# Gate and up of two pairs of 256 features in each FFN, as seven products of blocks in place of eight

## The chip, the core and the metric

The kernel runs on one core of a Trainium2 chip. The metric is the device time of one execution, in microseconds; it stands as the median of three runs. The engines are PE (TensorE: matmuls; PEld is its weight load), DVE (VectorE), ACT (ScalarE), POOL (GpSimd) and SP (SyncE, which issues most loads). Each engine works through its own instructions in the order of the program.

## What is computed

256 rows of 1024 features, in f32, go through an SSM layer, an attention layer and twice through FFN, hybrid mixer, FFN. The change is in the four FFNs, which are:

```python
D_FF = 2816
def swiglu(x, w_gate, w_up, w_down):
    return (jax.nn.silu(x @ w_gate) * (x @ w_up)) @ w_down
...
x = x + 0.5 * swiglu(rmsnorm(x, ffn1_norm[l]), ffn1_w_gate[l], ffn1_w_up[l], ffn1_w_down[l])
```

## The kernel before

**Products in three parts.** A weight is loaded as f32 ("raw"), and split into a high part (`whi`, an ACT cast to f32r) and a low part (`wlo = raw - whi`, a DVE subtraction). `mm3` (L195) forms one product as three matmuls, high x high, high x low, low x high.

**Weight units.** All weights of the layers after the SSM are cut into units of 1 MB (2048 elements in each of 128 partitions), in the order in which they are used. `converting` (L101) is a generator over them: a unit is split in four quarters, with a cast of 512 for each quarter and a low pass of 1024 for each two; a low pass is issued up to two passes late (`LAG`). Raw buffers are three, buffers of `whi` and of `wlo` four each. `lower` (L123) issues a low pass, and after a unit's last one `load` (L90) asks SP for the next unit.

**Slots.** `slot` (L153) issues one piece of PE's work, a list of tasks for the other engines, and conversions, in this order: the tasks, with 4 quarters (6 when behind) of conversion spread between them, and then the matmuls, with given PE tasks (transposes) at given places. `take` (L144) hands out the next unit and issues what is missing of it. `convert` stops when the units ready are three ahead of those taken (`if self.ready > self.taken + 2 - self.held: return`).

**An FFN** (`ffn`, L375) goes over 11 groups j of 256 features. For a group, `rows_of` (L187) takes two units, each with 512 of the 1024 inputs (four chunks of 128) and 256 columns of gate beside 256 of up: two slots of 24 matmuls of 128x512, into two PSUM banks `p[j][t]`, one for each 128 rows t. Then `gated` (L383: silu on ACT, L386, and a DVE product, L387), `turn` (L390: two transposes for each t, L394), and `divide` (L396: the split of the turned product `hh`, by ACT at L212 and DVE at L213). The down product of group j - 1 (`downs`, L408: one unit, 24 matmuls into four `acc` banks) is the third slot of group j; in it stand `gated` for both t and the transposes, with conversions between the two `gated`. The three matmuls of `mm3` are L199 to L201. `leave` (L276) adds a finished half to the rows. L74 and L79 are casts and low passes of 2048 elements in the SSM layer.

Of the kernel before, what the change touches and what calls it, by code (L numbers as in the profile page):

```python
# [26 lines left out]
LAG = 2  # L27


class Core:  # L30
# [52 lines left out]
    def plan(self, units):  # L83

        self.units = units
        self.raws, self.parts, self.lows = [], [], []
        self.taken = self.ready = self.done = self.held = 0
# [107 lines left out]
    def mm3(self, out, a, b, start, stop):  # L195

        nc = self.nc
        (ah, al), (bh, bl) = a, b
        nc.tensor.matmul(out, ah, bh, start=start, stop=False)  # L199
        nc.tensor.matmul(out, ah, bl, start=False, stop=False)  # L200
        nc.tensor.matmul(out, al, bh, start=False, stop=stop)  # L201
# [161 lines left out]

def ffn_units(w_gate, w_up, w_down):
    n = w_gate.shape[1] // 256
    out = []
    for j in range(n):
        cs = slice(j * 256, (j + 1) * 256)
        out += [(4, 512, [(0, w_gate[k * P:(k + 4) * P, cs]), (256, w_up[k * P:(k + 4) * P, cs])]) for k in (0, 4)]
        if j >= 1:  # L370
            out.append((2, D, [(0, w_down[(j - 1) * 256:j * 256, :])]))
    return out + [(2, D, [(0, w_down[(n - 1) * 256:n * 256, :])])]


def ffn(K, h, norm, n, nxt):  # L375


    nc = K.nc
    V = nc.vector
    p, hid, tp, parts, act = {}, {}, {}, {}, {}  # L380
    acc = []

    def gated(j, t):  # L383
        if t == 0:
            act[j], hid[j] = K.t([P, 2, 256], "act"), K.t([P, 2, 256], "hid")
        nc.scalar.activation(act[j][:, t], p[j][t][:, 0:256], AF.Silu, scale=norm.col[:, t:t + 1])  # L386
        V.scalar_tensor_tensor(hid[j][:, t], p[j][t][:, 256:512], norm.col05[:, t:t + 1], act[j][:, t], op0=ALU.mult,  # L387
                               op1=ALU.mult)

    def turn(j, t):  # L390
        if t == 0:
            tp[j] = K.psum("ps", [P, 2, 2, P], "tph")
        for k in range(2):
            nc.tensor.transpose(tp[j][:, k, t], hid[j][:, t, k * P:(k + 1) * P], K.ident)  # L394
# [17 lines left out]
    wait = []  # L412
    for j in range(n):
        p[j] = K.pair()
        for kh in range(2):
            tasks, pe = wait, []
            wait = []
# [4 lines left out]
            elif j == 1 and kh == 0:  # L422
                tasks = [lambda: gated(0, 0), lambda: gated(0, 1)]
                pe = [(5, lambda: turn(0, 0)), (7, lambda: turn(0, 1))]
                wait = [lambda: divide(0)]
            K.slot(K.rows_of(p[j], norm.x, K.take(), 4 * kh, 4, kh == 0, kh == 1), tasks, pe,
                   conv=2 if j == 0 and kh == 0 else 4)
        if j == 1:
            acc = [K.pair("acc", "acc") for _ in range(2)]
        if 1 <= j < n - 1:  # L430
            K.slot(downs(j - 1, K.take()), [lambda: gated(j, 0), lambda: gated(j, 1)],
                   [(3, lambda: turn(j, 0)), (5, lambda: turn(j, 1))])
            wait = [lambda j=j: divide(j)]
    j = n - 1
    w = [K.take()]
# [1498 lines left out]
```

## Time and profile before

| | us |
|---|---|
| median of three runs | 1413.04 (1410.56 to 1413.27) |
| the profiled execution, its own time | 1413.42 |
| its span, first to last instruction | 1411.3 |
| mean granted clock of TensorE, share of full speed | 0.992 |
| stretches of the four FFNs (us from the span's start) | 303 to 491, 663 to 851, 851 to 1039, 1211 to 1399 |

In the rows below, a line of the profile begins with the line of the code (L125), the engine and the operation, then out<-in by the names in the program, with the shape of each; "idle before" is the time in which the engine stood still just ahead of these instructions, and the arrow names what ended it.

### The profile page before, as it was taken

To read this page: it belongs to the slowest core of one execution; us is meant where nothing else is said; L and a number is where in the kernel's file an instruction comes from. 1 tells how busy PE (TensorE), PEld (TensorE's weight loads), DVE (VectorE), ACT (ScalarE), POOL (GpSimd) and SP (SyncE) were. 2 spreads that over 40 slices of the span, in tenths; PEclk is the share of its full clock that TensorE was granted. 3 is DMA by queue.
4 is the path that set the end of the run, shared out by engine and by line. 5 is a ranking of instruction groups with operands and counts; after the bars stand their busy time and mean duration, and the time that the engine had idled before them with its cause. 6 is when DMAs were issued, how large, how long until landed. Compare 5 with 4: busy or idle time off the path is not lost.

```text
span 1411.3 us, 21157 instructions
## 1 busy us (share of the span) xinstructions
PE 1381.1 (98%) x8301; PEld 1168.9 (83%) x8301; DVE 932.7 (66%) x1637; ACT 745.8 (53%) x1457; POOL 19.1 (1%) x35
## 2 busy tenths in 40 slices
PE   7988999999999999999999999999999999999996
PEld 6877888988888899887888888888899887888885
DVE  7889787675544589787554547554469987645444
ACT  6524667664444484565544446444457464644442
POOL 0002000000000000000000000000000000000000
PEclk9999999999999999999999999999999999999998
DMA  8233655365555444455655554655535445565550
GB/s 214 62 105 117 214 169 166 120 206 182 184 197 196 165 154 157 149 180 165 192 179 180 189 196 152 208 181 196 195 130 190 142 166 169 178 208 179 179 179 30
DMA packets 181348, 237.17 MB, mean 168 GB/s; under 512 B 16953, under 2 KB 140145, under 8 KB 181249
## 3 DMA queue, kind: packets, MB, share of 16 engines
q1 hardware_dynamic: 180160, 233.47, 51.3%
q0 software_dynamic: 672, 1.81, 0.4%
q8 instruction: 65, 1.06, 0.3%
q10 hardware_dynamic: 416, 0.55, 0.1%
q14 instruction: 35, 0.28, 0.1%
HBM read 234.76 MB, written 1.05 MB: 167 GB/s over the span
## 4 chain that ended last, share of the span: by engine, by line
PE 90%; DVE 6%; ACT 1%; issue 0%; DVEq 0%; ACTq 0%
PE p L199 19%; PE p L201 19%; PE p L200 19%; PE acc L199 6%; PE acc L201 6%; PE acc L200 6%; PE g L200 2%; PE g L199 2%; PE g L201 2%; PE tph L394 1%; PE lv L1502 1%; DVE m L769 1%; PE tp L288 1%; DVE S L773 1%; PE g L1025 1%; DVE m L771 1%
## 5 line engine op out<-in xcount | busy, mean ns | idle before, releaser
L113 ACT CAST whi<-raw 128x512 fp32r<-128x512 f32 x816 | 452.9, 618 | 290.1 <-PE p L201 237.3
L125 DVE TENSOR_TENSOR wlo<-raw,whi 128x1024 fp32r<-128x1024 f32 x408 | 483.7, 1216 | 0.3
L199 PE MATMUL p<-whi,xghi 128*128 128x512 f32 x960 | 380.1, 396 | 0.0
L201 PE MATMUL p<-whi,xglo 128*128 128x512 f32 x960 | 374.3, 390 | 0.0
L200 PE MATMUL p<-wlo,xghi 128*128 128x512 f32 x960 | 374.1, 390 | 0.0
L201 PEld LDWEIGHTS p<-whi,xglo 128*128 128x128 f32 x960 | 180.2, 188 | 38.7
L199 PEld LDWEIGHTS p<-whi,xghi 128*128 128x128 f32 x960 | 180.3, 188 | 36.3
L200 PEld LDWEIGHTS p<-wlo,xghi 128*128 128x128 f32 x960 | 180.5, 188 | 36.1
L387 DVE SCALAR_TENSOR_TENSOR hid<-p,col,act 128x256 f32<-128x256 f32 x88 | 42.5, 483 | 249.6 <-ACT act L386 249.6
L199 PE MATMUL acc<-whi,hh 128*128 128x512 f32 x352 | 145.8, 414 | 0.0
L200 PE MATMUL acc<-wlo,hh 128*128 128x512 f32 x352 | 138.2, 393 | 0.0
L201 PE MATMUL acc<-whi,hh 128*128 128x512 f32 x352 | 138.0, 392 | 0.0
L213 DVE TENSOR_TENSOR hh<-tph,hh 128x512 fp32r<-128x512 f32 x44 | 30.4, 691 | 89.7 <-ACT hh L212 89.7
L201 PEld LDWEIGHTS acc<-whi,hh 128*128 128x128 f32 x352 | 66.3, 188 | 16.4 <-DVE hh L213 1.7
L199 PEld LDWEIGHTS acc<-whi,hh 128*128 128x128 f32 x352 | 66.2, 188 | 12.4 <-ACT hh L212 1.7
L200 PEld LDWEIGHTS acc<-wlo,hh 128*128 128x128 f32 x352 | 66.4, 189 | 10.5
L199 PE MATMUL g<-xghi,whi 128*128 128x256 f32 x256 | 73.8, 288 | 0.0
L212 ACT CAST hh<-tph 128x512 fp32r<-128x512 f32 x44 | 25.8, 586 | 88.2 <-PE tph L394 88.2
L200 PE MATMUL g<-xglo,whi 128*128 128x256 f32 x256 | 72.4, 283 | 0.0
L201 PE MATMUL g<-xghi,wlo 128*128 128x256 f32 x256 | 72.4, 283 | 0.0
L554 PE MATMUL g<-xg,raw 128*128 128x256 f32 x256 | 62.2, 401 | 6.2 <-DVE kt L833 3.6
L554 PEld LDWEIGHTS g<-xg,raw 128*128 128x128 f32 x256 | 50.7, 202 | 14.3 <-DVE kt L833 3.9
(352 smaller groups left out, 1745.2 us busy)
## 6 DMA issues: line engine op xcount, KB each, us to landing
raw<-in_ffn_w_gate_dram SPq DMA_DIRECT2D x88, 512.0 KB, 4.0
raw<-in_ffn_w_up_dram SPq DMA_DIRECT2D x88, 512.0 KB, 5.1
raw<-in_ffn_w_down_dram SPq DMA_DIRECT2D x44, 1024.0 KB, 4.9
raw<-in_w_in_dram SPq DMA_DIRECT2D x36, 1024.0 KB, 5.1
raw<-in_attn_w_in_dram SPq DMA_DIRECT2D x16, 1024.0 KB, 5.6
raw<-in_w_out_dram SPq DMA_DIRECT2D x8, 1024.0 KB, 5.0
raw<-in_ssm_w_in_dram SPq DMA_DIRECT2D x7, 1024.0 KB, 5.7
raw<-in_ssm_w_glu_dram SPq DMA_DIRECT2D x4, 1024.0 KB, 5.2
```

The costliest lines, as they stand in the source:

```text
L113: self.nc.scalar.copy(hf[:, sl], raw[:, sl])
L125: self.nc.vector.tensor_tensor(out, raw, hi.bitcast(F32), op=ALU.subtract)
L199: nc.tensor.matmul(out, ah, bh, start=start, stop=False)
L200: nc.tensor.matmul(out, ah, bl, start=False, stop=False)
L201: nc.tensor.matmul(out, al, bh, start=False, stop=stop)
L212: self.nc.scalar.copy(hi, x)
L213: self.nc.vector.tensor_tensor(lo, x, hi.bitcast(F32), op=ALU.subtract)
L288: K.nc.tensor.transpose(self.tp[hf, c // 2][:, c % 2, t], self.h[:, t, k * P:(k + 1) * P], K.ident)
L387: V.scalar_tensor_tensor(hid[j][:, t], p[j][t][:, 256:512], norm.col05[:, t:t + 1], act[j][:, t], op0=ALU.mult, op1=ALU.mult)
L394: nc.tensor.transpose(tp[j][:, k, t], hid[j][:, t, k * P:(k + 1) * P], K.ident)
L554: nc.tensor.matmul(us[s][:, m], ws[s][:, k, m * P:(m + 1) * P], xg[:, k], start=k == 0, stop=k == KC - 1)
L769: V.tensor_tensor(m1, v, br, op=ALU.mult)
```

## The change

The 11 groups of an FFN become blocks 1, 1, 1, 2, 1, 2, 1, 1, 1 (`BLOCKS`). A block of 1 (`eight`) is as before. A block of 2 (`seven`) computes gate and up of two groups j and j + 1 for both halves of the rows from the four unit-sized blocks of the weights (two input halves times two groups) by Strassen's scheme in Winograd's form: seven products of a 128-row block (four chunks of 128 inputs, 12 matmuls) in place of eight.

- `Quad` describes the seven units of such a pair: four are loaded, into buffers of another pool (tag "e", with room for four), the third to the sixth are differences, which `add` writes by DVE subtractions of 1024 elements, one half ahead of the unit's turn and one at its start. All four loads are issued at the first unit's place. `load` now counts what is live, and goes on while there is room.
- `whole`, `mix`, `mixed_high`, `mixed_low`, once per FFN in blocks 1 and 2: x is put together again from its parts, four sums of its blocks are formed and split.
- `form` is one product; four of the seven add to a bank that holds an earlier one. `seven` copies the partial sums out (ACT), and adds (DVE: `sum11`, `sum12`, `sum22`) before `gated`.
- The down product of the group before stands between the fourth and the fifth and between the fifth and the sixth product, half and half.
- The block after a pair has two down products, with their transposes and `divide` in its first two slots.

`then(i, ...)` puts tasks into the i-th slot from the next on.

```diff
+ROOM = {"raw": 3, "e": 4}
...
+class Quad(list):
+    def __init__(self, b):
+        f = [Unit(4, 512, s, "e", ()) for s in (b[0][0], b[1][0], b[0][1], b[1][1])]
+        f += [Unit(4, 512, None, "e", ()) for _ in range(3)]
+        super().__init__(f)
+        f[2].sum = f[3].sum = ()
+        self[0].place = self.place
+    def place(self, loads):
+        n = len(loads)
+        f = self
+        for u in f[:4]:
+            loads.append((u.kc, u.cols, u.src, u.tag))
+            u.src = None
+        for u, need, raw, sub, frees in zip(f, (n, n + 1, n + 2, n + 3, n + 3, n + 3, n + 3),
+                                            (n, n + 1, n, None, n + 2, n + 1, n + 3),
+                                            (None, None, (n + 2, n), (n + 3, n), (n + 3, n + 2), (n + 1, f[3]), None),
+                                            (0, 0, 0, 1, 1, 1, 1)):
+            u.need, u.raw, u.sum, u.frees = need, raw, sub, ("e",) * frees
...
     def load(self):
         n = len(self.raws)
-        if n >= len(self.units):
-            self.raws.append(None)
-            return
-        kc, cols, srcs = self.units[n]
-        raw = self.wp.tile([P, kc, cols], F32, tag="raw", name=self.name("raw"), bufs=3)
+        if n >= len(self.loads):
+            return False
+        kc, cols, srcs, tag = self.loads[n]
+        if self.live[tag] >= ROOM[tag]:
+            return False
+        self.live[tag] += 1
+        if tag == "raw":
+            raw = self.wp.tile([P, kc, cols], F32, tag="raw", name=self.name("raw"), bufs=3)
+        else:
+            raw = self.e([P, kc, cols], "quad")
         for c, src in srcs:
             self.nc.sync.dma_start(raw[:, :, c:c + src.shape[1]], src.rearrange("(c p) n -> p c n", p=P))
         self.raws.append(raw)
+        return True
+    def add(self, i, half):
+        if i < len(self.units) and self.units[i].sum is not None:
+            u = self.units[i]
+            while len(self.raws) <= u.need:
+                assert self.load()
+            if u.raw is None and half == 0:
+                u.extra = self.big([P, u.kc, u.cols], "mixed")
+            sl = slice(half * 1024, half * 1024 + 1024)
+            a, b = (self.flat(x)[:, sl] for x in u.sum)
+            self.nc.vector.tensor_tensor(u.buffer(self)[:, sl], a, b, op=ALU.subtract)
+    def flat(self, x):
+        return x.buffer(self) if isinstance(x, Unit) else self.raws[x].rearrange("p c n -> p (c n)")
     def converting(self):
-        for i, (kc, cols, _) in enumerate(self.units):
-            while len(self.raws) <= max(i, 2):
-                self.load()
-            raw = self.raws[i].rearrange("p c n -> p (c n)")
-            hi, lo = (self.wp.tile([P, kc, cols], F32R, tag=t, name=self.name(t)) for t in ("whi", "wlo"))
+        while len(self.raws) < 3:
+            assert self.load()
+        for i, u in enumerate(self.units):
+            while len(self.raws) <= u.need:
+                assert self.load()
+            hi, lo = (self.wp.tile([P, u.kc, u.cols], F32R, tag=t, name=self.name(t)) for t in ("whi", "wlo"))
             self.parts.append((hi, lo))
             hf, lf = (x.rearrange("p c n -> p (c n)") for x in (hi, lo))
-            n = kc * cols // QUARTERS
+            n = u.kc * u.cols // QUARTERS
             for q in range(QUARTERS):
+                if q % 2 == 0:
+                    self.add(i + q // 2, 1 - q // 2)
+                raw = u.buffer(self)
                 sl = slice(q * n, (q + 1) * n)
                 self.nc.scalar.copy(hf[:, sl], raw[:, sl])
                 if q % 2:
                     sl = slice((q - 1) * n, (q + 1) * n)
-                    self.lows.append((lf[:, sl], raw[:, sl], hf[:, sl], q == QUARTERS - 1))
+                    self.lows.append((lf[:, sl], raw[:, sl], hf[:, sl], u if q == QUARTERS - 1 else None))
                 if len(self.lows) > LAG:
                     self.lower()
                 if q == QUARTERS - 1:
@@ -123,9 +201,12 @@
     def lower(self):
         out, raw, hi, last = self.lows.pop(0)
         self.nc.vector.tensor_tensor(out, raw, hi.bitcast(F32), op=ALU.subtract)
-        if last:
+        if last is not None:
             self.done += 1
-            self.load()
+            for tag in last.frees:
+                self.live[tag] -= 1
+            while self.load():
+                pass
...
+BLOCKS = (1, 1, 1, 2, 1, 2, 1, 1, 1)
...
+        if b == 1:
+            out += [(4, 512, quarter(j, k)) for k in (0, 4)] + down
+        else:
+            f = Quad([[quarter(j + i, k) for i in range(2)] for k in (0, 4)])
+            out += f[:4] + down[:1] + f[4:5] + down[1:] + f[5:]
...
+    def whole():
+        sums["f"] = K.big([P, 2, KC, T], "xs")
+        for hf in range(2):
+            ks = slice(4 * hf, 4 * hf + 4)
+            V.tensor_tensor(sums["f"][:, 0, ks], norm.x[0][:, ks].bitcast(F32), norm.x[1][:, ks].bitcast(F32), op=ALU.add)
+    def blocks():
+        f = sums["f"][:, 0]
+        f = [[f[:, 4 * hf:4 * hf + 4, t * P:(t + 1) * P] for hf in range(2)] for t in range(2)]
+        s = sums["f"][:, 1].rearrange("p (i k) (t q) -> p i (k t) q", i=4, q=P)
+        s = [s[:, i] for i in range(4)]
+        return f, s
+    def mix(i):
+        f, s = blocks()
+        a, b, op = ((f[1][0], f[1][1], ALU.add), (s[0], f[0][0], ALU.subtract), (f[0][0], f[1][0], ALU.subtract),
+                    (f[0][1], s[1], ALU.subtract))[i]
+        V.tensor_tensor(s[i], a, b, op=op)
+    def mixed_high():
+        sums["x"] = [K.e([P, 4, 4, P], n, F32R) for n in ("xshi", "xslo")]
+        nc.scalar.copy(sums["x"][0].rearrange("p i k q -> p (i k q)"), sums["f"][:, 1].rearrange("p c t -> p (c t)"))
+    def mixed_low():
+        hi, lo = (x.rearrange("p i k q -> p (i k q)") for x in sums["x"])
+        V.tensor_tensor(lo, sums["f"][:, 1].rearrange("p c t -> p (c t)"), hi.bitcast(F32), op=ALU.subtract)
+    def s_(i):
+        return [a[:, i] for a in sums["x"]]
+    def form(out, a, first=False):
+        w = K.take()
+        for k in range(4):
+            K.mm3(out, [y[:, k] for y in a], [y[:, k] for y in w], first and k == 0, k == 3, not first)
+            yield
...
+        places = (3, 5) if due else (5, 7)
+        then(0, lambda: gated(j, 0), lambda: gated(j, 1), pe=[(x, lambda t=t: turn(j, t)) for t, x in enumerate(places)])
+        then(1, lambda: divide(j))
+    def seven(j, due):
+        a, b, c = (K.psum("ps", [P, 512], "p") for _ in range(3))
+        c11, u2 = K.t([P, 512], "hid"), K.t([P, 512], "hid")
+        c22 = K.t([P, 512], "hid")
+        def sum11():
+            V.tensor_tensor(c11, c11, b, op=ALU.add)
+            gated(j, 0, c11)
+        def sum22():
+            V.tensor_tensor(c22, c22, a, op=ALU.add)
+            gated(j + 1, 1, c22)
+        def sum12():
+            V.tensor_tensor(u2, u2, c, op=ALU.add)
+            gated(j + 1, 0, u2)
+        def sum21():
+            p[j, 1] = a
+            gated(j, 1, a)
+        slot(form(a, x_(0, 0), first=True))
+        then(0, lambda: nc.scalar.copy(c11, a))
+        slot(form(b, x_(1, 0), first=True))
+        then(0, sum11)
+        slot(form(c, s_(0), first=True))
+        then(0, lambda: nc.scalar.copy(c22, c))
+        slot(form(a, s_(1)))
+        then(0, lambda: nc.scalar.copy(u2, a))
+        w = K.take()
+        K.held = 1
+        if len(due) == 1:
+            slot(downs(due[0], w, ((0, 0), (0, 1))))
+        else:
+            slot(downs(due[0], w))
+            K.held = 0
+        slot(form(a, s_(2)))
+        then(0, sum22)
+        if len(due) == 1:
+            slot(downs(due[0], w, ((1, 0), (1, 1))))
+            K.held = 0
+        else:
+            slot(downs(due[1], K.take()))
+        slot(form(a, x_(1, 1)))
+        then(0, sum21)
+        slot(form(c, s_(3)))
+        then(0, sum12, pe=[(2, lambda: turn(j, 0)), (2, lambda: turn(j, 1)), (4, lambda: turn(j + 1, 1)),
+                           (6, lambda: turn(j + 1, 0))])
+        then(1, lambda: divide(j), lambda: divide(j + 1))
+    j, due = 0, []
+    for b in BLOCKS[:-1]:
+        if b == 1:
+            eight(j, due)
+            if j == 0:
+                then(1, whole)
+            elif j == 1:
+                acc = [K.pair("acc", "acc") for _ in range(2)]
+                then(0, lambda: mix(0), lambda: mix(1))
+                then(1, lambda: mix(2), lambda: mix(3), mixed_high, mixed_low)
+            for d in due:
+                slot(downs(d, K.take()))
+        else:
+            seven(j, due)
+        due = list(range(j, j + b))
+        j += b
```

## Rows read from the trace of the kernel before

**Rows 1.** The page: its first line, and busy us (share of the span) of each engine

```profile
span 1411.3 us, 21157 instructions
PE 1381.1 (98%) x8301; PEld 1168.9 (83%) x8301; DVE 932.7 (66%) x1637; ACT 745.8 (53%) x1457; POOL 19.1 (1%) x35
```

**Rows 2.** The page's 40 slices: busy tenths of PE, its granted clock, the traffic

```profile
PE   7988999999999999999999999999999999999996
...
PEclk9999999999999999999999999999999999999998
...
GB/s 214 62 105 117 214 169 166 120 206 182 184 197 196 165 154 157 149 180 165 192 179 180 189 196 152 208 181 196 195 130 190 142 166 169 178 208 179 179 179 30
```

**Rows 3.** Windows: each FFN, busy us of each engine, granted clock, DMA share, GB/s

```profile
core 0: us, PE busy (x) PEld busy (x) DVE busy (x) ACT busy (x) POOL busy (x), PEclk, DMA share, GB/s
303.00:491.00 188.00, 188.00 (x855) 154.05 (x854) 99.14 (x120) 89.52 (x173) 0.00 (x0) 1.00 0.57 184
663.00:851.00 188.00, 188.00 (x855) 154.06 (x854) 99.13 (x120) 90.80 (x174) 2.04 (x4) 1.00 0.57 185
851.00:1039.00 188.00, 188.00 (x854) 153.88 (x853) 101.11 (x125) 92.96 (x183) 0.00 (x0) 1.00 0.56 185
1211.00:1399.00 188.00, 187.98 (x849) 153.64 (x847) 95.39 (x117) 87.10 (x168) 0.00 (x0) 1.00 0.50 162
```

**Rows 4.** Timeline of PE in one FFN (start, us); first and last of 18, transposes

```profile
699.86 0.39 PE L199 MATMUL p<-whi,xghi 128*128 128x512 f32 x1
...
703.71 0.39 PE L201 MATMUL p<-whi,xglo 128*128 128x512 f32 x1
...
706.43 0.40 PE L201 MATMUL acc<-whi,hh 128*128 128x512 f32 x1
706.66 0.38 PE L394 MATMUL tph<-ident,hid 128*128 128x128 f32 x2
...
707.12 0.40 PE L200 MATMUL acc<-wlo,hh 128*128 128x512 f32 x1
```

**Rows 5.** Groups by line: count, busy us, mean ns, idle before

```profile
L125 DVE TENSOR_TENSOR wlo<-raw,whi 128x1024 fp32r<-128x1024 f32 x408 | 483.7, 1216 | 0.3
L113 ACT CAST whi<-raw 128x512 fp32r<-128x512 f32 x816 | 452.9, 618 | 290.1 <-PE p L201 237.3 <-PE acc L201 30.9 <-DMA raw<-in_ffn_w_up_dram 4.9
...
L387 DVE SCALAR_TENSOR_TENSOR hid<-p,col,act 128x256 f32<-128x256 f32 x88 | 42.5, 483 | 249.6 <-ACT act L386 249.6
L386 ACT ACTIVATE act<-p,rs 128x256 f32<-128x256 f32 x88 | 41.4, 471 | 28.9 <-PE p L201 28.0 <-ACT whi L113 0.6
...
L213 DVE TENSOR_TENSOR hh<-tph,hh 128x512 fp32r<-128x512 f32 x44 | 30.4, 691 | 89.7 <-ACT hh L212 89.7
L212 ACT CAST hh<-tph 128x512 fp32r<-128x512 f32 x44 | 25.8, 586 | 88.2 <-PE tph L394 88.2
...
L79 DVE TENSOR_TENSOR wlo<-raw,whi 128x2048 fp32r<-128x2048 f32 x8 | 18.3, 2305 | 2.1 <-ACT whi L74 2.1
L74 ACT CAST whi<-raw 128x2048 fp32r<-128x2048 f32 x8 | 15.2, 1912 | 33.9 <-DMA raw<-in_ssm_w_glu_dram 33.9
L276 DVE TENSOR_TENSOR h<-acc,h 128x512 f32<-128x512 f32 x16 | 11.0, 688 | 12.0 <-PE acc L201 12.0
```

**Rows 6.** Timeline of DVE and of ACT in the same FFN

```profile
701.92 0.48 DVE L387 SCALAR_TENSOR_TENSOR hid<-p,col,act 128x256 f32<-128x256 f32 x1 [4.22 <-ACT act L386]
702.33 1.22 DVE L125 TENSOR_TENSOR wlo<-raw,whi 128x1024 fp32r<-128x1024 f32 x1
...
709.31 0.69 DVE L213 TENSOR_TENSOR hh<-tph,hh 128x512 fp32r<-128x512 f32 x1 [1.97 <-ACT hh L212]
709.92 4.62 DVE L125 TENSOR_TENSOR wlo<-raw,whi 128x1024 fp32r<-128x1024 f32 x4
...
701.42 0.47 ACT L386 ACTIVATE act<-p,rs 128x256 f32<-128x256 f32 x1 [0.49 <-PE p L201]
...
710.13 2.18 ACT L113 CAST whi<-raw 128x512 fp32r<-128x512 f32 x4 [0.86 <-PE acc L201]
```

**Rows 7.** Waits of SP's queue, 690 to 830 us

```profile
SPq L98 <- DVE wlo L125: 123.0, 26, 9.2
```

**Rows 8.** The page's DMA issues: KB each, median us from issue to landing

```profile
raw<-in_ffn_w_gate_dram SPq DMA_DIRECT2D x88, 512.0 KB, 4.0
raw<-in_ffn_w_up_dram SPq DMA_DIRECT2D x88, 512.0 KB, 5.1
raw<-in_ffn_w_down_dram SPq DMA_DIRECT2D x44, 1024.0 KB, 4.9
```

**Rows 9.** Waits of PE's weight loads in the FFN from 663 to 851 us

```profile
PEld acc L201 <- DVE hh L213: 0.4, 1, 0.4
PEld acc L199 <- ACT hh L212: 0.4, 1, 0.4
```

More of the change, by code (lines that the diff above doesn't have):

```diff
@@ L27, with __init__, buffer, place @@
 LAG = 2
+ROOM = {"raw": 3, "e": 4}
+class Unit:
+    def __init__(self, kc, cols, src=None, tag="raw", frees=("raw",)):
+        self.kc, self.cols, self.src, self.tag, self.frees = kc, cols, src, tag, frees
+        self.sum = self.raw = self.extra = None
+        self.need = -1
+    def place(self, loads):
+        if self.src is not None:
+            loads.append((self.kc, self.cols, self.src, self.tag))
+            self.need = len(loads) - 1
+            if self.sum is None:
+                self.raw = self.need
+    def buffer(self, K):
+        return (self.extra if self.raw is None else K.raws[self.raw]).rearrange("p c n -> p (c n)")
+class Quad(list):
[5 more added lines that the diff above has]
+        self[0].place = self.place
+    def place(self, loads):
+        n = len(loads)
[8 more added lines that the diff above has]
+            u.need, u.raw, u.sum, u.frees = need, raw, sub, ("e",) * frees
 class Core:
@@ L83, in plan @@
     def plan(self, units):
-        self.units = units
+        self.units = [u if isinstance(u, Unit) else Unit(*u) for u in units]
+        self.loads = []
+        for u in self.units:
+            u.place(self.loads)
         self.raws, self.parts, self.lows = [], [], []
+        self.live = {"raw": 0, "e": 0}
         self.taken = self.ready = self.done = self.held = 0
@@ L193, in rows_of, with mm3 @@
                 yield
-    def mm3(self, out, a, b, start, stop):
+    def mm3(self, out, a, b, start, stop, more=False):
         nc = self.nc
         (ah, al), (bh, bl) = a, b
-        nc.tensor.matmul(out, ah, bh, start=start, stop=False)
-        nc.tensor.matmul(out, ah, bl, start=False, stop=False)
-        nc.tensor.matmul(out, al, bh, start=False, stop=stop)
+        nc.tensor.matmul(out, ah, bh, start=start, stop=False, skip_group_check=more)
+        nc.tensor.matmul(out, ah, bl, start=False, stop=False, skip_group_check=more)
+        nc.tensor.matmul(out, al, bh, start=False, stop=stop, skip_group_check=more)
     def pair(self, tag="ps", name="p"):
@@ L361, in out_project, with quarter @@
             nxt.leave(hf, t, acc[t])
+BLOCKS = (1, 1, 1, 2, 1, 2, 1, 1, 1)
 def ffn_units(w_gate, w_up, w_down):
-    n = w_gate.shape[1] // 256
-    out = []
-    for j in range(n):
+    def quarter(j, k):
         cs = slice(j * 256, (j + 1) * 256)
[L369 to L372, printed above, removed]
+        return [(0, w_gate[k * P:(k + 4) * P, cs]), (256, w_up[k * P:(k + 4) * P, cs])]
+    out, j, due = [], 0, []
+    assert sum(BLOCKS) == w_gate.shape[1] // 256 and BLOCKS[:2] == BLOCKS[-2:] == (1, 1)
+    for b in BLOCKS:
+        down = [(2, D, [(0, w_down[d * 256:(d + 1) * 256, :])]) for d in due]
+        if b == 1:
[5 more added lines that the diff above has]
+        j += b
+    return out + [(2, D, [(0, w_down[d * 256:(d + 1) * 256, :])]) for d in due]
 def ffn(K, h, norm, n, nxt):
@@ L379, in ffn, with slot, then, gated @@
     V = nc.vector
-    p, hid, tp, parts, act = {}, {}, {}, {}, {}
+    p, hid, tp, parts = {}, {}, {}, {}
     acc = []
[L383 to L388, printed above, removed]
+    ahead = [([], []) for _ in range(3)]
+    def slot(mm, tasks=(), pe=(), **kw):
+        t, x = ahead.pop(0)
+        ahead.append(([], []))
+        K.slot(mm, t + list(tasks), x + list(pe), **kw)
+    def then(i, *tasks, pe=()):
+        ahead[i][0].extend(tasks)
+        ahead[i][1].extend(pe)
+    def gated(j, t, src=None):
+        s = p[j][t] if src is None else src
+        o = K.t([P, 512], "hid") if src is None or src is p.get((j, t)) else src
+        a, hid[j, t] = o[:, 0:256], o[:, 256:512]
+        nc.scalar.activation(a, s[:, 0:256], AF.Silu, scale=norm.col[:, t:t + 1])
+        V.scalar_tensor_tensor(hid[j, t], s[:, 256:512], norm.col05[:, t:t + 1], a, op0=ALU.mult, op1=ALU.mult)
     def turn(j, t):
-        if t == 0:
+        if j not in tp:
             tp[j] = K.psum("ps", [P, 2, 2, P], "tph")
         for k in range(2):
-            nc.tensor.transpose(tp[j][:, k, t], hid[j][:, t, k * P:(k + 1) * P], K.ident)
+            nc.tensor.transpose(tp[j][:, k, t], hid[j, t][:, k * P:(k + 1) * P], K.ident)
     def divide(j):
@@ L410, in downs, with x_, eight @@
             yield from down(j, w, hf, t)
-    wait = []
-    for j in range(n):
+    sums = {}
+    def x_(hf, t):
+        return [a[:, 4 * hf:4 * hf + 4, t * P:(t + 1) * P] for a in norm.x]
+    def whole():
[27 more added lines that the diff above has]
+            yield
+    def eight(j, due):
         p[j] = K.pair()
         for kh in range(2):
-            tasks, pe = wait, []
-            wait = []
+            tasks, pe = [], []
             if j == 0 and kh == 0:
@@ L421, in ffn @@
                 tasks = [norm.col_, norm.half_col]
[L422 to L433, printed above, removed]
+            slot(K.rows_of(p[j], norm.x, K.take(), 4 * kh, 4, kh == 0, kh == 1), tasks, pe,
+                 conv=2 if j == 0 and kh == 0 else 4)
+        places = (3, 5) if due else (5, 7)
+        then(0, lambda: gated(j, 0), lambda: gated(j, 1), pe=[(x, lambda t=t: turn(j, t)) for t, x in enumerate(places)])
@@ new lines, in ffn @@
+    j, due = 0, []
[12 more added lines that the diff above has]
+            seven(j, due)
+        due = list(range(j, j + b))
+        j += b
@@ L434, in ffn @@
     j = n - 1
+    eight(j, due)
+    ahead[0] = ([], [])
+    ahead[1] = ([], [])
     w = [K.take()]
```

## The prediction

> **What bounds the kernel now.** I read the page's busy shares first, then the slices, then one FFN by windows, then single instructions of it. TensorE (PE) is busy for 1381 of 1411 us, VectorE (DVE) for 933 [rows 1], and the granted clock is at full speed, 2.4 GHz, in almost every slice, also in the early ones where PE is busy for only eight tenths [rows 2]; so I put no price on the clock for short waits of PE. Each of the four FFNs is a stretch of 188 us in which PE is never idle while DVE works for 95 to 101 us and ScalarE (ACT) for 87 to 93 [rows 3]. There PE starts a matmul of 512 columns every 3.85 us / 17 = 0.2265 us [rows 4]. So today the number of matmuls sets the time of an FFN, and the splitting of weights (DVE, ACT) is cover.
>
> The profiled execution took 1413.42 us, 2.1 more than its span of 1411.3, and 0.4 more than the median of 1413.04; the sum starts from 1413.4. Up to 0.2%, 2.8 us, I count as no change.
>
> **What goes.** A pair of feature groups now needs 2 x 48 = 96 matmuls for gate and up, and would need 7 products x 4 chunks x 3 = 84. Twelve fewer per pair, 24 x 0.2265 = 5.44 us per FFN, 21.7 us in all. All of it is on the path, since PE is never idle there. The Trainium skill (TensorE: Matmul & The Clock Gate, Back-to-back issue gap) gives about 131 ns per 512-column matmul in a sustained stream; by that the saving would be 96 x 0.131 = 12.6 us, an estimate from that page. Rows 4 disagree with it, and the sum uses their 0.2265.
>
> **What comes, on DVE and ACT.** One pass of DVE over 1024 elements takes 1.22 us alone and 1.133 in a row ((4.62 - 1.22)/3); a cast of 512 on ACT takes 0.62 alone, 0.52 in a row ((2.18 - 0.62)/3) [rows 5, 6]. The new subtractions have the shape of the present low part (two f32 tiles in SBUF, 1024 elements), so I price them as that. A pair was 4 weight units and becomes 7: 6 more low passes, 12 more casts; four of the units are differences of others: 8 passes. So DVE gets 14 x 1.133 = 15.9 us per pair, and three additions from PSUM, as the 0.69 us of L276, 0.61 in a row by L213 [rows 5, 6]: together 17.7. Once per FFN come `whole` (2 passes), four `mix` (512 elements, 0.61) and `mixed_low` (2048 elements, 2.3 by L79 [rows 5]): 7.0. An FFN then has DVE work of 99 + 35.4 + 7.0 = 141 of 183 us; ACT, with 24 casts (12.5), six copies of 0.59 as L212 (3.5) and a cast of 1.9 (L74), has 90 + 18 = 108. On average everything still fits. The question is where in the pair it falls.
>
> **Slot by slot through a pair.** Call the seven weight units U1 to U7, their products F1 to F7 (12 matmuls, 2.72 us each), and the two halves of the down product between them D and D' (12 each). U3 to U6 are differences. The order is written by the program, each engine keeps it, and `form` takes its unit only after the slot's conversions have been issued, so in a pair conversions run two units ahead, not three as in the other slots. Written out, this stands on DVE behind `sum11` (the addition that needs F2's result): the lows of U4 (2), the subtractions for U5 (2), the lows of the down weight (2), the subtractions for U6 (2), the lows of U5 (2): ten passes, all ahead of F5's second half, because chunks 2 and 3 of F5 need U5's last low.
>
> Let T be the end of F2 on PE. DVE has by then done what stands before `sum11` and waits about 1 us for it. `sum11` starts at T + 0.2 (a matmul's end lies 0.16 after the next one's start [rows 4], a handover is 0.03 [rows 6]). Addition 0.69, silu on ACT 0.47, two handovers, the gating multiply 0.41: T + 1.83. Ten passes: 9 x 1.133 + 1.22 = 11.42, and a handover: T + 13.28. PE would reach the middle of F5 after F3, F4, D and half of F5, 42 matmuls: T + 9.51. **So PE waits 3.8 us**, spread over F4, D and F5. ACT has some 8 us of casts in those 13 and follows. After F5 `sum22` must wait for F5 and stands ahead of U6's lows: 0.15 more before F6. That is 3.95 per pair, against 2.72 saved. Bounds of 3.95: with every pass at 1.22 (no overlap), 4.8; without the waits of DVE for F2 and for silu (1.7), 2.2.
>
> **Around the pairs.** *The mixing of x in blocks 1 and 2.* From the second slot of block 1 to the second gating of block 2, DVE has 14 passes (15.9 us), four mixes (2.4), `mixed_low` (2.2), two `divide` (1.2) and four gatings (1.6): 23.3 us, starting 2.4 ahead. PE wants that gating's transposes after 20.2 us. A hold of 0 to 1.5; I take 0.5.
>
> *After the second pair.* Only three raw buffers exist, and SP's queue already waits for DVE's last low before each load [rows 7]. During a pair no raw buffer is used up after its down weight, so the three then hold block 8's two quarters of gate/up and its first down weight; the fourth load starts only when DVE, late from the pair, has split the first of them, about 0.8 us into block 8. A down weight lands 4.9 us after its issue, a gate/up quarter 0.4 + 5.1 [rows 8]. In the program's order the rest follows: fourth load in at 5.7, its first two casts on ACT (1.04), `divide` of the pair on ACT and DVE (0.59 + 0.03 + 0.61), the last low of the first down weight (1.22): 9.2. That frees the buffer for the unit whose casts stand on ACT between the two silus of block 8; it lands at 14.7, and casts, silu and gating (1.04 + 0.47 + 0.48 and two handovers) end at 16.8. The transposes that need them are due on PE at 15.4 (24 + 24 + 15 matmuls and five pairs of transposes at 0.23 [rows 4]). A hold of 1.4, between 0 (quicker loads) and 3 (a load that lands 1.6 late behind the others); I take 1.5. After the first pair the next loads are the second pair's, which need no raw buffer: 0.1, counted as nothing.
>
> *At nothing:* the bytes are the same. A pair's four loads (4 MB, 20 us at the 214 GB/s of the fullest slice [rows 2]) are asked for some four slots of 5.44 before F1 and land one by one; were that cover gone, PE would wait up to 5 us per pair. The extra casts lie in ACT's idle half. The copies of partial sums (0.59) are issued at least one slot of 2.72 before their bank is written again. The transposes and gatings keep their number.
>
> **The sum.** Per FFN: -5.44 + 2 x 3.95 + 0.5 + 1.5 = +4.46; four FFNs: +17.8. 1413.4 + 17.8 = 1431.2, said as 1431. With the low bounds -5.44 + 4.4 = -1.0 per FFN, 1409; with the high ones -5.44 + 9.6 + 1.5 + 3 = +8.7, 1448.
>
> **Rivals.** *The work fits (faster).* DVE at 141 of 183 us leaves slack. If DVE reaches F3 with enough done, because the lookahead built up before the pair holds, the holds vanish and the 21.7 us are won: 1391.7. For it: PE waited for DVE only twice by 0.4 us in a whole FFN [rows 9]. Against it: four buffers of each part let no conversion start more than three units ahead, and `sum11` pins the ten passes behind F2 however early DVE is; this rival needs the wait there below 2.7 us per pair and the other holds gone. The Trainium skill (Perfetto Trace Analysis, Identifying the Most-Contended Engine) would have the engine with the highest occupancy relieved first; that rule speaks for this rival, with PE at 98% and DVE at 66% [rows 1], and the same page's Optimization Strategy grants that the most-contended engine can change over time.
>
> *Half hidden.* Holds of 1 to 2.2 per pair and little around: 1396 to 1409.
>
> *Heavier (slower still).* If a matmul has to wait for its unit's whole low part and not for the half it reads, F5 starts only at T + 13.28 where it was due at T + 8.16: 5.1 instead of 3.8, similarly at F6: some 2 us more per pair, 16 in all, 1449. Against it: in L199 to L201 the down product waits for ACT's half of `hh` and for DVE's half at different matmuls [rows 9], so parts of a tile are followed separately.
>
> **How the numbers follow.** Forecast, with its bounds 1409 to 1448: 0.72. All hidden, near 1392: 0.12. Half hidden: 0.07. Heavier, 1449 and up: 0.09. The range 1405 to 1450 leaves out about 0.2 of this. Within 2.8 us of before lies the lower end of the forecast, 0.06; faster are the two hidden cases and the forecast's lowest edge, 0.2; slower is what remains, 0.74.
>
> **What the next profile would show.** Right: 84 and not 96 product matmuls per pair; in the timeline of a pair PE idle before matmuls of F4, D and F5, released by DVE's low parts (L125's successor), 3 to 5 us in all; DVE dense from `sum11` to U5's last low; at the end of the second pair transposes that wait for the gating multiply, and casts released by a DMA; the FFN's stretch some 192 us. The spacing of matmuls stays 0.227, the clock full. Wrong: an FFN stretch below 188 us with PE without gaps (the first rival), passes of the subtractions well off 1.13 us, or long waits for the pair's loads.

## The result, and the profile after

The changed kernel takes 1431.8 us (median of four runs, 1428.89 to 1432.99) against 1411.8 for the kernel before, measured beside it (1410.2 to 1413.27): ratio 1.0139, 95% interval 1.0118 to 1.016. It is slower by 20.0 us; 17.8 were forecast. The profiled execution took 1432.99 us with a span of 1431.0, 19.7 more than the span before.

The page of the kernel after: span, busy times, and the shares of the chain that ended last, by engine.

```profile
span 1431.0 us, 21193 instructions
...
PE 1377.9 (96%) x8205; PEld 1151.2 (80%) x8205; DVE 1103.0 (77%) x1801; ACT 814.4 (57%) x1581; POOL 28.1 (2%) x35
...
PE 79%; DVE 12%; DMA 2%; issue 2%; ACT 2%; SPq 0%; DVEq 0%; ACTq 0%
```

96 matmuls fewer, and PE's busy time fell by 3 us only [rows 1]. Most of that is the waits: a matmul that stands alone beside one is busy for 0.39 to 0.50 us, in a row one starts every 0.227; in run 10 below, where these waits are gone, it falls by 20.5. Some matmuls also ran at half clock (below). DVE has 170 us more work. It is still far from full, yet the chain that ended last now runs through it for 12% of the span. The views below say where. First the waits of PE: line waited for, then us in total, times, longest.

```profile
PE acc L281 <- DVE wlo L203: 15.4, 16, 1.3
PE p L281 <- DVE wlo L203: 4.8, 8, 0.6
...
PE tph L498 <- DVE hid L492: 2.0, 3, 0.8
```

Sixteen waits in the down products (`acc`) and eight in the products of blocks (`p`): two and one in each of the eight pairs, always for a low part (L203, the former L125). The timeline of DVE in the second pair of the second FFN shows what it did meanwhile (start, duration, engine and line, operation, idle time before). F3 starts on PE at 772.81; that is T.

```profile
773.09 0.69 DVE L581 TENSOR_TENSOR hid<-hid,p 128x512 f32<-128x512 f32 x1 [1.67 <-PE p L282]
774.35 0.48 DVE L492 SCALAR_TENSOR_TENSOR hid<-hid,col 128x256 f32<-128x256 f32 x1 [0.58 <-ACT hid L491]
774.75 1.22 DVE L203 TENSOR_TENSOR wlo<-mixed,whi 128x1024 fp32r<-128x1024 f32 x1
775.89 1.22 DVE L168 TENSOR_TENSOR quad<-quad,quad 128x1024 f32<-128x1024 f32 x1
...
782.70 1.22 DVE L168 TENSOR_TENSOR quad<-quad,mixed 128x1024 f32<-128x1024 f32 x1
783.84 2.35 DVE L203 TENSOR_TENSOR wlo<-quad,whi 128x1024 fp32r<-128x1024 f32 x2
787.92 0.69 DVE L585 TENSOR_TENSOR hid<-hid,p 128x512 f32<-128x512 f32 x1 [1.73 <-PE p L282]
```

DVE is idle for 1.67 us, because `sum11` (L581) stands next in its queue and F2 has not ended. It waits 0.58 us more for the silu, and then works through the gating and ten passes without a gap, to 786.19, which is T + 13.38 (predicted T + 13.28). The same stretch on PE, second half of F4, D, and F5 up to its second half:

```profile
776.03 0.50 PE L281 MATMUL p<-wlo,xshi 128*128 128x512 f32 x1
...
778.30 0.50 PE L281 MATMUL p<-wlo,xshi 128*128 128x512 f32 x1 [0.61 <-DVE wlo L203]
...
780.57 0.50 PE L281 MATMUL acc<-wlo,hh 128*128 128x512 f32 x1 [0.61 <-DVE wlo L203]
...
782.84 0.50 PE L281 MATMUL acc<-wlo,hh 128*128 128x512 f32 x1 [1.31 <-DVE wlo L203]
...
784.80 0.40 PE L280 MATMUL p<-whi,xshi 128*128 128x512 f32 x1
785.11 0.50 PE L281 MATMUL p<-wlo,xshi 128*128 128x512 f32 x1
...
786.59 0.39 PE L281 MATMUL p<-wlo,xshi 128*128 128x512 f32 x1
```

Each of the first four, and the one at 785.11, starts on the end of a low pass. F5 starts at 784.80; 36 matmuls after T it was due at 772.81 + 8.16 = 780.97. So PE lost 3.83 us here, 0.2 to 0.3 more up to F6, and 0.33 more in F6, whose first low part stands behind `sum22`: 4.4 per pair. The tenth pass, from which the prediction took the hold, stopped nothing: it ends at 786.19, and the matmul that reads it starts 0.40 later, in its regular turn. PE had been held by the passes before it, by 3.7 us already at the last wait in D (782.84, due at 779.16). The tenth pass would have held it by about as much, so the number comes out alike.

**Half clock.** In one pair of each FFN there is more. A table of stretches (busy us and instructions of each engine; PEclk is the granted clock as a share of 2.4 GHz):

```profile
729.70:732.70 3.00, 3.00 (x8) 2.34 (x7) 2.98 (x3) 1.14 (x2) 0.00 (x0) 0.50 0.71 213
720.00:729.00 9.00, 6.67 (x26) 4.25 (x24) 8.42 (x9) 6.60 (x13) 0.00 (x0) 1.00 0.01 3
364.90:367.90 3.00, 3.00 (x8) 2.33 (x8) 3.00 (x3) 1.14 (x2) 0.00 (x0) 0.53 0.78 218
975.80:978.80 3.00, 3.00 (x9) 2.37 (x8) 2.34 (x3) 1.14 (x2) 0.00 (x0) 0.52 0.98 322
1340.60:1343.60 3.00, 3.00 (x8) 2.31 (x7) 3.00 (x3) 1.14 (x2) 0.00 (x0) 0.50 0.69 220
```

In the 9 us before 729 the clock is full, but PE, with the waits of such a pair, is busy for 6.67 of 9.00 us. Then, right after the longest wait of the pair, the lower level (1.2 GHz) holds for some 3 us, and matmuls start 0.43 us apart. Two of them from the timeline of PE, with the one that waited:

```profile
729.33 0.65 PE L281 MATMUL acc<-wlo,hh 128*128 128x512 f32 x1 [1.31 <-DVE wlo L203]
729.78 0.63 PE L282 MATMUL acc<-whi,hh 128*128 128x512 f32 x1
730.20 0.63 PE L280 MATMUL acc<-whi,hh 128*128 128x512 f32 x1
```

In these four pairs some seven matmuls cost 0.2 us more each; F5 is late by 5.0 to 5.3 us instead of 3.8, and the end of the pair by 5.6 to 5.8 instead of 4.4, so about 1.3 us per FFN. The executions differ in the same way: the one with a mean granted clock of 0.993 took 1428.89 us, the three with 0.989 or 0.990 took 1431.77 to 1432.99.

**After the second pair** the transposes wait for the gating (0.40 to 1.1 us, mean 0.76 over the FFNs). Here the chain behind one of them, a cast on ACT, the gating's two steps, and the transposes on PE:

```profile
811.15 1.14 ACT L191 CAST whi<-raw 128x512 fp32r<-128x512 f32 x2 [1.84 <-DMA raw<-in_ffn_w_up_dram]
812.19 0.47 ACT L491 ACTIVATE hid<-p,rs 128x256 f32<-128x256 f32 x1
...
812.69 0.48 DVE L492 SCALAR_TENSOR_TENSOR hid<-p,col,hid 128x256 f32<-128x256 f32 x1 [0.80 <-ACT hid L491]
...
813.23 0.44 PE L498 MATMUL tph<-ident,hid 128*128 128x128 f32 x2 [0.58 <-DVE hid L492]
```

Casts that wait for a load stand on ACT ahead of the silu; DVE and PE inherit the delay.

Per FFN this makes -5.44 + 2 x 4.4 + 1.3 + 0.76 = +5.4, for four 21.7. From first product to last, the stretches that hold the FFNs grew by 21.1 us (4.8 for the first, 10.7 for the second and third, 5.6 for the fourth); what lies ahead of the first and behind the last took 1.4 us less in this execution, and so the spans differ by 19.7.

### The profile page after: what moved, and what is told of

Same layout as the page of the kernel before. It is cut to its first block, busy times and chain, and to the rows that moved or that the text cites. A ratio compares the mean times of both kernels' runs of the same rounds, so it can differ in the third digit from the quotient of the medians.

```text
span 1431.0 us, 21193 instructions
## 1 busy us (share of the span) xinstructions
PE 1377.9 (96%) x8205; PEld 1151.2 (80%) x8205; DVE 1103.0 (77%) x1801; ACT 814.4 (57%) x1581; POOL 28.1 (2%) x35
## 4 chain that ended last, share of the span: by engine, by line
PE 79%; DVE 12%; DMA 2%; issue 2%; ACT 2%; SPq 0%; DVEq 0%; ACTq 0%
PE p L280 15%; PE p L281 15%; PE p L282 15%; PE acc L281 5%; PE acc L282 5%; PE acc L280 5%; DVE wlo L203 4%; PE g L281 2%; PE g L280 2%; PE g L282 2%; DVE quad L168 2%; DMA raw<-in_ffn_w_up_dram 1%; PE lv L1712 1%; PE tph L498 1%; PE g L764 1%
## 5 line engine op out<-in xcount | busy, mean ns | idle before, releaser
L191 ACT CAST whi<-raw 128x512 fp32r<-128x512 f32 x688 | 381.7, 619 | 151.3 <-PE p L282 81.7
L203 DVE TENSOR_TENSOR wlo<-raw,whi 128x1024 fp32r<-128x1024 f32 x344 | 410.5, 1217 | 7.6 <-ACT whi L191 7.2
L280 PE MATMUL p<-whi,xghi 128*128 128x512 f32 x800 | 319.9, 400 | 0.0
L281 PE MATMUL p<-wlo,xghi 128*128 128x512 f32 x800 | 312.8, 391 | 0.3
L282 PE MATMUL p<-whi,xglo 128*128 128x512 f32 x800 | 312.5, 391 | 0.0
L281 PEld LDWEIGHTS p<-wlo,xghi 128*128 128x128 f32 x800 | 150.5, 188 | 32.6 <-DVE wlo L203 3.6
L282 PEld LDWEIGHTS p<-whi,xglo 128*128 128x128 f32 x800 | 150.2, 188 | 32.1
L281 PE MATMUL acc<-wlo,hh 128*128 128x512 f32 x352 | 141.8, 403 | 15.4 <-DVE wlo L203 15.4
L191 ACT CAST whi<-quad 128x512 fp32r<-128x512 f32 x192 | 107.9, 617 | 52.3 <-DVE quad L168 29.7
L203 DVE TENSOR_TENSOR wlo<-quad,whi 128x1024 fp32r<-128x1024 f32 x96 | 113.6, 1217 | 0.0
L492 DVE SCALAR_TENSOR_TENSOR hid<-p,col,hid 128x256 f32<-128x256 f32 x64 | 30.8, 481 | 68.7 <-ACT hid L491 68.6
```

The lines of the kernel that those rows point to most:

```text
L280: nc.tensor.matmul(out, ah, bh, start=start, stop=False, skip_group_check=more)
L281: nc.tensor.matmul(out, ah, bl, start=False, stop=False, skip_group_check=more)
L282: nc.tensor.matmul(out, al, bh, start=False, stop=stop, skip_group_check=more)
L492: V.scalar_tensor_tensor(hid[j, t], s[:, 256:512], norm.col05[:, t:t + 1], a, op0=ALU.mult, op1=ALU.mult)
```

## The experiments

The theory: `sum11` pins the passes behind it to the end of F2, and so it is the order on DVE's queue that costs time. The rivals: DVE simply has too much work in the pair; the mixing, or the loads, carry the loss. All runs were timed in rounds against the kernel before, which took 1411.0 to 1411.3 us there (1411.8 beside the kernel after); ratios are to it, and the diffs are against the kernel after (1431.8).

**1. `sum11` one slot later.** By the theory, a later place leaves fewer passes behind it that PE needs soon.

```diff
-        then(0, sum11)
+        then(1, sum11)
```

> sum11 with its gating is issued one slot later (in the slot of F4, no longer at the start of F3's); nothing else is changed. Theory (the order on DVE: ten passes stand behind an addition that waits for F2): DVE no longer idles for F2's end, so the chain starts up to 2.2 us earlier, but sum11 still stands in it; the hold of PE in a pair falls from 3.5 by about 1 us, 8 pairs, 1421 to 1426 us. Rival (the total of DVE's work in the pair sets the hold, the place of sum11 does not matter): 1430 to 1433. Rival (the products in their new form cost the time): 1430 to 1433.

1421.15 us, ratio 1.0068 (1.0048 to 1.0087). The waits in F4 are gone, those in D remain:

```profile
PE acc L281 <- DVE wlo L203: 16.8, 16, 1.3
```

This is the line that stood at 15.4 before the edit; the `p` line has vanished. Moving one addition without taking any work away is worth 10.7 us.

**2. The eight subtractions left out.** The four difference units are split from loaded blocks instead.

```diff
-                                            (n, n + 1, n, None, n + 2, n + 1, n + 3),
-                                            (None, None, (n + 2, n), (n + 3, n), (n + 3, n + 2), (n + 1, f[3]), None),
+                                            (n, n + 1, n, n + 3, n + 2, n + 1, n + 3),
+                                            (None,) * 7,
```

> The eight subtractions of a pair's weight blocks are left out: the units that should be differences are split from a loaded block as it is; PE's and ACT's work and the loads stay. Theory (DVE's passes hold PE): 8 x 1.13 = 9.1 us less on DVE per pair, so the holds of about 3.5 and the restarts behind them vanish and the 21.7 us of removed matmuls show: 1393 to 1401 us, with no stretch of half clock in the pairs. Rival (the products in their new form, with sums over two banks, are what is slow): 1425 to 1432, DVE idle and PE still behind.

1398.3 us, ratio 0.9908 (0.9891 to 0.9924). No wait for a low part is left, and the clock has no dip in the two FFNs read:

```profile
303.00:490.00 187.00, 186.30 (x857) 151.76 (x856) 126.03 (x151) 108.76 (x213) 2.13 (x4) 1.00 0.56 186
660.00:845.00 185.00, 184.39 (x835) 149.47 (x834) 124.93 (x149) 108.49 (x210) 0.00 (x0) 1.00 0.57 188
```

So the loss lies on DVE, not in the loads, which this kernel still makes. But fewer passes fit the theory and the rival of too much work alike.

**3. The new code without pairs.** All weights go through the new queues and slots; x is still mixed, and no pair uses it.

```diff
-BLOCKS = (1, 1, 1, 2, 1, 2, 1, 1, 1)
+BLOCKS = (1,) * 11
```

> All blocks are of one group (eight products for each pair, as in the kernel before), but x is still put together, mixed and split once per FFN as in the changed kernel. Theory (mixing costs 0 to 1.5 us per FFN): 1411 to 1418 us. Rival (the work around the pairs, not the pairs, takes a large part of the loss): 1420 or more.

1411.17 us, ratio 1.0 (0.9991 to 1.001). The mixing and the rewritten conversion cost nothing that can be measured: the loss is all in and behind the pairs.

**4. The subtractions on GpSimd.** POOL is idle; if a pass there were as quick as on DVE, DVE's load would fall as in run 2.

```diff
-            self.nc.vector.tensor_tensor(u.buffer(self)[:, sl], a, b, op=ALU.subtract)
+            self.nc.gpsimd.tensor_tensor(u.buffer(self)[:, sl], a, b, op=ALU.subtract)
```

> The eight subtractions of a pair run on GpSimd in place of DVE; order and data stay. Theory (DVE's passes hold PE): with GpSimd taking at most some 2.7 us for 128x1024 it hides them and the time is as without them, 1394 to 1404 us. No row shows such a pass on GpSimd (the nearest, 128x32, took 1.27 us); at 5 us each it would itself hold PE, 40 us per pair against 25, and the time would be 1440 to 1530. Rival (products in the new form are slow): not below 1425 in either case.

1460.66 us, ratio 1.0353 (1.0337 to 1.0368). Groups of this kernel by form, one of POOL and two of DVE:

```profile
L168 POOL TENSOR_TENSOR quad<-quad,quad 128x1024 f32<-128x1024 f32 x32 | 97.8, 3076 | 701.1 <-ACT whi L191 455.1 <-DVE wlo L203 119.5 <-DMA quad<-in_ffn_w_up_dram 63.9
...
L203 DVE TENSOR_TENSOR wlo<-quad,whi 128x1024 fp32r<-128x1024 f32 x96 | 165.8, 1771 | 0.0
L203 DVE TENSOR_TENSOR wlo<-mixed,whi 128x1024 fp32r<-128x1024 f32 x16 | 53.5, 3383 | 0.0
```

The same two groups of DVE in the kernel after:

```profile
L203 DVE TENSOR_TENSOR wlo<-quad,whi 128x1024 fp32r<-128x1024 f32 x96 | 113.6, 1217 | 0.0
...
L203 DVE TENSOR_TENSOR wlo<-mixed,whi 128x1024 fp32r<-128x1024 f32 x16 | 19.5, 1218 | 0.0
```

A pass takes 3.1 to 3.4 us on POOL in the mean. And the low passes of DVE that run beside one take up to 3.38 us instead of 1.22: these two groups grew by 52 and 34 us, more than the 78 (64 x 1.22) that DVE was to be spared. PE's waits in the products of blocks grew from 4.8 to 35.6 us:

```profile
PE p L281 <- DVE wlo L203: 35.6, 17, 4.2
```

The Trainium skill (SBUF — State Buffer, SBUF: two separate sides) says that DVE operations with two SBUF inputs and GpSimd operations that read SBUF take turns at one pair of ports, each holding it for a whole instruction. These rows agree: where passes of both kinds run in a row, each takes 3.38 us, near the sum of POOL's quickest pass (2.40) and one of DVE (1.13 in a row), so that each holds a wait for the other. The quickest pass stands in the durations (ns, least, median, greatest) of one group:

```profile
L168 POOL TENSOR_TENSOR quad<-quad,quad x32: 2401/3304/3387, 339.0 to 1358.9; 128x1024 f32<-128x1024 f32 x32
```

The expectation that 2.7 us or less would be hidden left these turns out.

**5 and 6. The same extra work ahead of `sum11` and behind it.** Three additions of 512 elements per pair, into a tile not yet in use; one place is tasks of F2's slot, the other the task after `sum11`. This tells order from amount: if DVE had too much work, both should cost the same.

```diff
+        def extra():
+            x = norm.x[0][:, 0:2].bitcast(F32).rearrange("p k t -> p (k t)")
+            for _ in range(3):
+                V.tensor_tensor(u2, x, x, op=ALU.add)
...
-        then(0, lambda: nc.scalar.copy(c11, a))
+        then(0, lambda: nc.scalar.copy(c11, a), extra)
```

> Three additions of 512 elements (3 x 0.61 = 1.83 us of DVE, with a result that nothing uses) are added to each pair, issued in F2's slot, ahead of sum11. Theory (sum11 is pinned to F2's end, and DVE waited 1.2 to 3.1 us for it, 16.1 us over the eight pairs): the work fits into that wait but for some tenths in three pairs: 1431 to 1434 us. Rival (the total of DVE's work in a pair sets the hold): 8 x 1.83 = 14.6 us more, 1443 to 1449.

1433.47 us, ratio 1.0151 (1.0136 to 1.0166), 1.7 more than without the extra, and the two intervals overlap. DVE's wait for F2 fell from 16.1 us over the eight pairs to 0.8; first line the kernel after, second this one:

```profile
DVE hid L581 <- PE p L282: 16.1, 8, 3.1
```

```profile
DVE hid L581 <- PE p L282: 0.8, 4, 0.3
```

Behind `sum11`:

```diff
-        then(0, sum11)
+        then(0, sum11, extra)
```

> The same three additions, issued right behind sum11's gating. Theory: they lengthen the queue that F5's second half waits for, 8 x 1.83 = 14.6 us more: 1443 to 1449. Rival (DVE is not what PE waits for in the pair, or has slack there): 1430 to 1434.

1446.64 us, ratio 1.0244 (1.0226 to 1.0262), 14.8 more than the kernel after. The extra in the timeline of DVE, PE's waits in the products, and the start of F5 in that pair (T is 723.06):

```profile
726.13 2.13 DVE L599 TENSOR_TENSOR hid<-xghi 128x512 f32<-128x512 f32 x3
```

```profile
PE p L281 <- DVE wlo L203: 21.3, 8, 2.7
```

```profile
737.09 0.39 PE L280 MATMUL p<-whi,xshi 128*128 128x512 f32 x1
```

2.05 us more of DVE per pair (three at a spacing of about 0.68) are 16.4 in eight pairs; 14.8 of it arrive in the time. F5 starts at T + 14.03; in the pair of the kernel after it was T + 11.99, so it comes later by just the length of the extra. The same additions are nearly free ahead of the addition that waits and cost almost their whole length behind it. The rival of too much work falls.

**7. Each product takes its unit before its slot.** Conversions then run three units ahead in a pair too, and more passes stand ahead of `sum11`.

```diff
-        w = K.take()
+        return products(K.take(), out, a, first)
+
+    def products(w, out, a, first):
+
```

> A product of the pair takes its unit before its slot is issued, not inside, so that conversions run three units ahead in the pairs too; nothing else. Theory (order on DVE): U4's passes move ahead of sum11 into DVE's wait, so fewer than ten stand behind it; about 4 us per FFN less: 1411 to 1419 us. Rival (the total of DVE's work): 1429 to 1433.

1407.07 us, ratio 0.9971 (0.996 to 0.9983), below what was expected. In the pair read from its trace seven passes stand behind `sum11` ahead of F5's second half, not ten, and the wait in F4 is gone; those in the down product were halved:

```profile
PE acc L281 <- DVE wlo L203: 8.3, 9, 1.3
```

**8 and 10. Also `sum11` behind `sum22`,** the addition that waits for F5; run 8 with low passes issued one pass late instead of two (`LAG = 1`), run 10 without that. Run 10's edit, beside that of run 7:

```diff
-        then(0, sum11)
...
-        then(0, sum22)
+        then(0, sum22, sum11)
```

> Units taken before the slot, sum11 with its gating moved behind sum22 (after F5), and low passes issued at most one pass late in place of two. DVE then has nothing that waits for PE between the pair's begin and F5. Theory: no hold of more than some tenths is left, the removed matmuls show: 1390 to 1399 us, faster than the kernel before. Rival (DVE's total work of some 35 us in a pair's 25 holds PE in any order): 1410 or more.

> As in the eighth experiment (units before the slot, sum11 behind sum22), but with low passes up to two late, as in both kernels. If the place of units and of sum11 gave its gain, the time is within 3 us per FFN of it: 1397 to 1409 us; if issuing the low passes sooner gave most of it, it is near the run with the unit taken first alone: 1405 to 1409.

Run 8: 1396.34 us, ratio 0.9892 (0.9878 to 0.9907). Run 10: 1395.27 us, ratio 0.9884 (0.9868 to 0.9901), a little below its expected 1397. The lag makes no difference; the place of `sum11` does: the units taken sooner gave 24.7 us (run 7), and `sum11` behind `sum22` 11.8 more. `sum11` moved without the sooner units was tried by one slot only (run 1). Run 10's page and its waits of PE in the FFNs:

```profile
span 1394.5 us, 21201 instructions
...
PE 1360.6 (98%) x8205; PEld 1151.0 (83%) x8205; DVE 1102.0 (79%) x1801; ACT 815.0 (58%) x1581; POOL 27.6 (2%) x35
```

```profile
PE p L280 <- ACT hid L605: 4.2, 7, 0.7
...
PE acc L281 <- DVE wlo L203: 0.6, 1, 0.6
```

DVE does the same 1801 instructions in the same 1102 us of busy time as in the kernel after, and the kernel is 36.5 us quicker. In DVE's timeline nothing waits for F2 any more; it reaches `sum22` (L588) just as F5 ends, and `sum11` (L584) follows:

```profile
765.47 4.62 DVE L203 TENSOR_TENSOR wlo<-quad,whi 128x1024 fp32r<-128x1024 f32 x4
770.33 0.69 DVE L588 TENSOR_TENSOR hid<-hid,p 128x512 f32<-128x512 f32 x1 [0.24 <-PE p L282]
771.60 0.48 DVE L492 SCALAR_TENSOR_TENSOR hid<-hid,col 128x256 f32<-128x256 f32 x1 [0.58 <-ACT hid L491]
772.00 0.68 DVE L584 TENSOR_TENSOR hid<-hid,p 128x512 f32<-128x512 f32 x1
```

What is left is seven waits of PE for ACT's copy of a partial sum (L605), 4.2 us in all. This version beats both kernels, by 1.2% and 2.6%.

**9. The waits filled.** Twelve matmuls of 512 columns per pair into a spare PSUM bank, at the places where PE waits: 96 in all, as many as the change removes. DVE's order is that of the kernel after; `fill(n)` issues n of them.

```diff
-        slot(form(a, s_(1)))
+        slot(form(a, s_(1)), pe=[(1, lambda: fill(3)), (3, lambda: fill(3))])
...
-            slot(downs(due[0], w, ((0, 0), (0, 1))))
+            slot(downs(due[0], w, ((0, 0), (0, 1))), pe=[(0, lambda: fill(6))])
```

> Twelve matmuls of 512 columns per pair with a result that nothing uses are put where PE waits: three ahead of the third chunk of F4, three ahead of D, six ahead of D's second chunk (2.7 us of PE, where it waits about 3.5). Theory (the half clock in some pairs follows from these waits, and costs some 1.5 us each time): no stretch of half clock left in the pairs, 1422 to 1428 us, although PE has 96 more matmuls. Rival (the half clock has another cause): clock and time as in the changed kernel, 1430 to 1434. Rival (PE does not in truth wait there): 96 x 0.227 = 21.8 us more, 1448 or more.

1427.9 us, ratio 1.0118 (1.0103 to 1.0133), 3.9 less than the kernel after although PE does 96 matmuls more. The stretch from the first FFN to the last, first the kernel after, then this one:

```profile
283.00:1419.00 1136.00, 1111.64 (x5517) 916.45 (x5515) 863.63 (x1214) 651.43 (x1249) 6.30 (x11) 0.99 0.52 172
```

```profile
283.00:1413.00 1130.00, 1125.54 (x5607) 929.18 (x5606) 862.51 (x1212) 651.24 (x1248) 6.30 (x11) 1.00 0.53 172
```

With PE busy in the pairs the granted clock stays full in all four FFNs. So the dips come from PE's waits, and cost the kernel after about 4 us by the medians, whose intervals overlap in part; the count from its timeline says 5.

## Why the prediction was right, and which terms were not

The sign, the place and nearly the size were right: 1431.8 for 1431.2. That the two agree to 0.6 us is luck: the sum starts from one execution at 1413.4 where the median was 1411.8, so the change itself is 20.0 for 17.8, and errors of both signs went into that. Point by point:

- **Saved matmuls, -5.44 per FFN:** the count fell from 8301 [rows 1] to 8205, 96 in all, and the spacing at full clock is 0.227. The trace of after disagrees, as that of before did, with the 131 ns that the prediction quotes from the Trainium skill (TensorE: Matmul & The Clock Gate, Back-to-back issue gap).
- **A pass costs 1.133 in a row:** the subtractions start 1.13 to 1.14 us apart and take 1.22, like the low passes.
- **The hold, 3.95 per pair:** 4.4. The chain pinned to T ended within 0.1 us of the forecast, and waits fell in F4, D and at F5, released by low passes. The last wait of size is in D, though, not at F5's second half, as shown above. Around `sum22` the sum had 0.15, and 0.5 to 0.6 came. At full clock PE needs about 0.1 more than the pure wait to get going again (0.33 to 0.34 us to the next matmul instead of 0.227), which was not in the sum. Runs 5, 6 and 10 show the mechanism itself, the order on DVE.
- **DVE's wait for F2, "about 1 us":** 16.1 us over eight pairs, 2.0 each. DVE was further ahead than I had counted; that changes nothing, since `sum11` starts with F2's end in either case (run 5 spends that time at almost no cost).
- **Mixing, 0.5 per FFN:** about nothing. Run 3 costs nothing, and in the FFN after that was read gap by gap, blocks 1 and 2 hold 0.13 us of it.
- **Behind the second pair, 1.5:** 0.76, half the size, by the mechanism described (load, cast, silu, gating, transposes).
- **"So I put no price on the clock for short waits of PE": the step that failed.** It was drawn from slices with PE at eight tenths and a clock of nine tenths [rows 2], read as full; but a 9 there begins at 0.90, and the mean of 35 us hides a short dip. In one pair of each FFN of the kernel after the clock fell to half for 3 us: 4 to 5 us in all. The clock and the larger hold were 2.2 us too cheap per FFN; mixing and the stretch behind the pair were 0.5 and 0.74 too dear, which cancels about half of it. The trace before had such dips already: from 106 to 142 us, where PE is busy for 88%, its mean clock was 0.95, and this stretch lies in it, beside waits of PE of 0.70, 1.01 and 1.40 us between 117 and 122 us:

```profile
121.60:124.90 3.30, 2.88 (x108) 2.88 (x112) 3.23 (x6) 0.31 (x1) 1.06 (x2) 0.50 0.06 7
```

- **The rivals.** That everything fits fell as this kernel is ordered: 1431.8, not 1391.7. Its premise, slack on DVE, was true, though: in the order of run 10 the same work takes 1395.27, 3.6 us from that figure. The row given for it shows one wait for DVE and one for ACT, both of weight loads [rows 9]. The rule cited for it, in the Trainium skill (Perfetto Trace Analysis, Identifying the Most-Contended Engine), judges TensorE's headroom by its weight loads, 83% in [rows 1], not by the 98% of its matmuls; PE is highest either way. Waits for whole tiles (by 16 us dearer, so 1447, not the 1449 given) were not seen: F5 starts before its unit's second half is split (784.80 against 786.19).

## What to carry to other kernels

An operation that waits for the bottleneck engine pins everything behind it in its queue to that moment; before adding work to an engine with slack on average, write out what stands behind each such operation and who needs it when. Here the same instructions in another order turned a loss of 20 us into a gain of 16. Where an addition's own result isn't urgent, put it behind the work that is, and start splitting ahead before the slot rather than in it.

## What the runs showed of the hardware beyond that

- The granted clock fell to half for some 3 us after waits of PE of only 0.6 to 1.3 us, in four of eight pairs with the same kind of waits; filled with matmuls, the pairs kept the full clock (run 9). Which pairs it hits is not fixed by the kernel: in run 5, whose waits are alike, it is three of the eight, and not all of them the same (at 729, 924 and 1289 us of its trace). What decides between the two sorts of pairs stays open.
- A subtraction of 128x1024 in f32 takes 2.4 us at the quickest on GpSimd, 3.1 to 3.4 in the mean beside DVE's passes, and those stretch from 1.22 to as much as 3.38 (run 4): GpSimd is no relief for DVE here.
